# Softmax weights of both attentions turned by VectorE and moved through HBM, with the values a unit later

## The chip, the cores and the metric

One NeuronCore of a Trainium2 chip runs the kernel alone. The metric is device microseconds of one launch. The engines are named as in the profile: PE is TensorE, DVE is VectorE, ACT is ScalarE, POOL is GpSimd, SP is SyncE, whose queue issues nearly all DMAs here. Every engine, SP included, runs its own instructions strictly in the order in which the program was built: an instruction that waits holds back all that stands behind it on that engine.

## The reference

Two layers, 256 tokens, model width 1024, float32. In each layer the input is normalised, multiplied by one wide matrix, and given to three token mixers; a squared-ReLU MLP follows.

```python
for l in range(DEPTH):                                    # DEPTH = 2
    h = rms_norm(x, attn_norm[l])
    x = x + hybrid_mixer(h, ...)
    h = rms_norm(x, mlp_norm[l])
    x = x + squared_relu_mlp(h, w_mlp_up[l], w_mlp_down[l])
return rms_norm(x, final_norm)

# hybrid_mixer
p = h @ w_in
(cq, ckv, k_rope, mq, mk, mv, rq, rk, rv, rg, g_mla, g_moba, g_ret) = split(p)
o_mla  = mla_branch(cq, ckv, k_rope, ...)       # causal softmax attention, 8 heads
o_moba = moba_branch(mq, mk, mv, ...)           # with 256 tokens one block: causal softmax attention, 8 heads
o_ret  = retention_branch(rq, rk, rv, rg, ...)  # 4 heads, decay in place of softmax, group norm
merged = (sigmoid(g_mla) * (o_mla @ w_branch_mla) + sigmoid(g_moba) * (o_moba @ w_branch_moba)
          + sigmoid(g_ret) * (o_ret @ w_branch_ret))
return merged @ w_out
```

An attention head needs its softmax weights with the keys on the partitions before they can be multiplied with the values: the weights have to be turned.

## The kernel before

**Weights.** All weights stream from HBM in blocks of 512 KB (a unit): SP issues the load of `raw`, ACT rounds it to `whi` (L222), DVE subtracts to `wlo` (L224), and PE multiplies in three passes (L243 to L245), 12 matmuls of 128x512 to a unit. There are 7 buffers of `raw` and 6 each of `whi` and `wlo`. The order of the units is the plan in `weight_plan`; the names used here are those of the plan: `gmla`, `gmoba`, `gret` are the gates of the three mixers (two halves of four units each, `gmoba1.2` being the third unit of the second half), `bmla`, `bmoba`, `bret` the branch matrices (two units to a half), `rqk` (four units), `rv` and `rg` the retention's projections.

**Accumulators.** PE has four banks for `acc` and for the attention's output `po` together, taken in turn, so a unit that opens a new accumulator waits for the engine that empties the one four places earlier; and four banks for scores and the like.

**Attention.** Each attention is worked in two groups of four heads. For a group PE makes the scores `ps_s`; DVE masks and takes the maximum (L524, L527), ACT takes the exponent (L533), DVE divides (L536, L538). Then the weights `prob` are turned, by one of two ways:

- in blocks: DVE turns each head in 32x32 squares (`turned_blocks`, L543) and 16 DMAs of 48 KB, SBUF to SBUF, put the squares in place (`moved_blocks`, L594). They all stand on SP's queue, but for the second group of MoBA, where 8 stand on ACT's queue;
- on PE: `turn` (L549) makes three transposes to a head against the identity into `ps_pt`, and ACT copies the result (L550).

The first group of the MLA attention and both groups of MoBA take the first way, the second group of MLA the second. PE then multiplies with the values (`po`, L609 and L611), and ACT and DVE split the result into `omlah`, `omlal` or `omobah`, `omobal` (L264).

**Where things stand.** A list of slots says after which unit each such job is written: `first`, `gap` and `turn` of `attention` count units from the attention's first slot. The engine order within that is made when the program is built. In layer 0 of the kernel before, PE runs gmoba0.2, the 12 transposes, gmoba0.3, gmoba1.0, gmoba1.1, the MLA values together with the first MoBA scores, gmoba1.2, gmoba1.3, bmla (four units), rqk.0, rqk.1, the second MoBA scores, rqk.2, rqk.3, rv, rg.0 to rg.3, the MoBA values with the retention's scores `ps_r`, then gret. The last matmul of rg.3 stands behind `ps_r`. Layer 1 is the same some 402 us later. `retA` (L1034) is the retention's scores times their decay table `dec`, `por` its output, `gn` its norm's weights, loaded by SP (L1101), `qkoth` a moved copy of queries or keys for the rotation (L464, DMAs, and POOL or DVE at L476 and L479).

Of the kernel before, what the change touches and what calls it, by code (L numbers as in the profile page):

```python
# [7 lines left out]
F32 = mybir.dt.float32  # L8
# [6 lines left out]
P = 128  # L15
D = 1024
S = 256
# [45 lines left out]
def weight_plan():  # L63

    plan = []

    def block(key, name, kt, cols, per):
        for j in range(0, kt, per):
            plan.append(((*key, j // per), name, (j, per), cols))

    def turned(key, cols):
        for n in range(4):
            block((*key, n), "w_in", KD, cols[P * n : P * n + P], KD)

    def span(c, n):
        return range(c, c + n)

    for l in range(L):
        if l == 0:

            for i in range(2):
                plan.append(((l, "mq", i), "w_in", (0, 1), C_MQ[256 * i : 256 * i + 256]))
            plan.append(((l, "b0", 0), "w_in", (0, 1), C_MLA))
            for k in range(1, KD):
                plan.append(((l, "b0mq", k), "w_in", (k, 1), [*C_MLA, *C_MQ]))
        else:
            block((l, "b0"), "w_in", KD, C_MLA, 2)
            turned((l, "mq"), C_MQ)
        turned((l, "mk"), C_MK)
        block((l, "mv"), "w_in", KD, C_MV, 2)  # L90
        mv, plan = plan[-4:], plan[:-4]
        for i, (key, name, kt, cols) in enumerate(
            (("qrope", "mla_w_q_up", 2, C_QROPE), ("qnope", "mla_w_q_up", 2, C_QNOPE), ("kvup", "mla_w_kv_up", 1, C_KV))
        ):
            block((l, key), name, kt, cols, kt)
            plan.append(mv[i])
        plan.append(mv[3])
        for i in range(2):
            block((l, "gmla%d" % i), "w_in", KD, span(C_GMLA + 512 * i, 512), 2)
        for i in range(2):  # L100
            block((l, "gmoba%d" % i), "w_in", KD, span(C_GMOBA + 512 * i, 512), 2)
        def branch_block(name, i):
            block((l, "b%s%d" % (name, i)), "w_branch_" + name, 4, span(512 * i, 512), 2)

        for i in range(2):
            branch_block("mla", i)
        turned((l, "rqk"), C_RQK)
        block((l, "rv"), "w_in", KD, C_RV, 2)
        block((l, "rg"), "w_in", KD, span(C_RG, 512), 2)
        for i in range(2):  # L110
            block((l, "gret%d" % i), "w_in", KD, span(C_GRET + 512 * i, 512), 2)
        for name, i in LATE:
            branch_block(name, i)
        for n in range(KD):
            block((l, "wout", n), "w_out", KD, span(P * n, P), KD)
        for kind, i in mlp_order():
            if kind == "up":
                g, j = divmod(i, 4)
                plan.append(((l, "up", g, j), "w_mlp_up", (2 * j, 2), span(512 * g, 512)))
            else:  # L120
                plan.append(((l, "down", i, 0), "w_mlp_down", (i, 1), range(D)))
    at, offset = {}, 0
# [26 lines left out]
def trunk(ctx: ExitStack, tc: tile.TileContext, gx, wts, consts, gfin, gn, xtok, out):  # L149
# [83 lines left out]
    def misc_tile(name="misc"):  # L233
        return ps.tile([P, 512], F32, name=name, tag="misc", bufs=4)
# [281 lines left out]
    def attention_head(scale):  # L516


        got = {}

        def scores(s_ps):
            p = sb.tile([P, 3 * P], F32, name="prob", bufs=4)
            m = small("smx")
            nc.vector.tensor_tensor_reduce(  # L524
                p[:, 0:P], s_ps[:, 0:P], mask[:, P : 2 * P], 1.0, NEG_INF, ALU.add, ALU.max, m[:, 0:1]
            )
            nc.vector.tensor_tensor_reduce(  # L527
                p[:, P : 3 * P], s_ps[:, P : 3 * P], mask, 1.0, NEG_INF, ALU.add, ALU.max, m[:, 1:2]
            )
            nc.vector.tensor_scalar(m[:, 2:4], m[:, 0:2], -scale, None, op0=ALU.mult)  # L530
            spans = ((0, P), (P, 3 * P))
            for i, (a, b) in enumerate(spans):
                nc.scalar.activation(  # L533
                    p[:, a:b], p[:, a:b], AF.Exp, bias=m[:, 2 + i : 3 + i], scale=scale, accum_out=m[:, 4 + i : 5 + i]
                )
            nc.vector.reciprocal(m[:, 6:8], m[:, 4:6])  # L536
            for i, (a, b) in enumerate(spans):
                nc.vector.tensor_scalar(p[:, a:b], p[:, a:b], m[:, 6 + i : 7 + i], None, op0=ALU.mult)  # L538
            got["p"] = p

        def turn_blocks(dst):

            return nc.vector.transpose(dst, got["p"])  # L543

        def turn(dst):

            pt = misc_tile("ps_pt")
            for i, src in enumerate((0, P, 2 * P)):
                nc.tensor.transpose(pt[:, P * i : P * i + P], got["p"][:, src : src + P], ident)  # L549
            return lambda: nc.scalar.activation(dst, pt[:, : 3 * P], AF.Copy)  # L550

        return scores, turn_blocks, turn

    def attention(oT, vs, scale, first, group, former, gap, turn, homes):

# [5 lines left out]
        def four_tile(h):  # L561
            if h // 4 not in tiles:
                tiles[h // 4] = sb.tile([P, 4 * 3 * P], F32, name="probT", bufs=2)
            return tiles[h // 4]
# [12 lines left out]
                tc.keep_in_program_order(turning)  # L577
            pT[h] = o[:, 0:2], o[:, 2]

        def turned(h):  # L580

            o = four_tile(h)[:, 3 * P * (h % 4) : 3 * P * (h % 4) + 3 * P]
            pT[h] = o[:, 0:S], o[:, S : 3 * P]
            return heads[h][2](o)

        def moved_blocks(h0):


            e = 3 * P
            for a in range(4):  # L590
                for b in range(4):
                    src = pT["blocks"][32 * a : 32 * a + 32, e * b : e * b + e]
                    queue = nc.scalar if h0 and b % 2 else nc.sync
                    dma = queue.dma_start(four_tile(h0)[32 * b : 32 * b + 32, e * a : e * a + e], src)  # L594
                    if former:
                        tc.keep_in_program_order(dma)

        def values(h0):

# [27 lines left out]
        at(first, lambda: in_a_row(*former, lambda: four(0)))  # L627
        at(first + gap, lambda: in_a_row(lambda: four(4)))
        for i in range(2):
            if homes[i] is None:  # L630
                at(first + turn[i], lambda i=i: in_a_row(*(lambda h=h: turned(h) for h in range(4 * i, 4 * i + 4))))
                continue
            for h in range(4):
                at(first + turn[i] + h // 2, lambda h=4 * i + h: turned_blocks(h, heads[h][1]))
            at(first + turn[i] + 1, lambda i=i: moved_blocks(4 * i))
# [91 lines left out]
    def at(slot, step):  # L727
        steps.setdefault(slot, []).append(step)
# [12 lines left out]
    def layer(l, xn, before):  # L741
# [222 lines left out]
        def mla_scores(h0):  # L964
# [3 lines left out]
                    nc.tensor.matmul(bank[:, o], mla["Q"][:, h, qs], mla["K"][:, h, ks], start=True, stop=True)  # L968
            return banks

        mla_last = attention(
            omlaT, lambda: mla["v"], QKD**-0.5, first, mla_scores, (), MLA_GAP, MLA_TURN, ("probT", None)
        )


# [3 lines left out]
        def load_dec():  # L979

            rqkv["dec"] = sb.tile([P, K_TURNED_MB - K_DEC], F32, name="dec", tag="Q", bufs=1)
            tc.keep_in_program_order(nc.sync.dma_start(rqkv["dec"], consts[:, K_DEC:K_TURNED_MB]))

        at(slot("gmoba1", 3), load_dec)
        merged, mT = {}, []
        branch(l, "bmla", range(2), omlaT, th_mla, merged)
        if l == 0:

            for i, (key, j) in enumerate((("gmoba0", 0), ("gmoba0", 1), ("gmoba1", 0), ("gmoba1", 1))):
                at(slot(key, j), lambda i=i: moba_rope(("mk", "mq")[i % 2], i // 2))  # L990
        first = slot("gmoba1", 1)
        at(first, lambda: omobaT.extend((t4("omobah"), t4("omobal"))))

        def moba_scores(h0):
# [6 lines left out]
            return banks  # L1001

        moba_last = attention(
            omobaT, lambda: mqkv["mv"], MB_D**-0.5, first, moba_scores, mla_last, GAP, TURN, ("KK", "KK")
        )


# [74 lines left out]
                split_turned(oret_T[0], oretT)  # L1082

        project_turned(l, "rqk", xn, ret_pair)
        project(l, "rv", xn, 512, ret_done("rv"))


# [38 lines left out]
        branches = {"moba": (omobaT, th_moba), "ret": (oretT, th_ret)}  # L1126
        for name, half in LATE:
            branch(l, "b" + name, [half], *branches[name], merged, between if name == "ret" else None)
        at(slot("rg", 1), lambda: in_a_row(*moba_last, ret_scores))
        for h in range(RT_H):  # L1130
            at(slot("rg", 3), lambda h=h: ret_values(h))
        at(slot("rg", 3), group_norm)
        at(slot("rg", 3), oret_blocks)
        at(slot("bmoba1", 1), oret_split)


# [235 lines left out]
GAP = 8  # L1372
# [87 lines left out]
```

## Time and profile before

| what | value |
|---|---|
| median of 3 runs | 815.7 us (815.59 to 816.0) |
| profiled execution | 816.03 us |
| its span | 814.1 us |
| granted TensorE clock | 0.999 |
| PE busy | 807.1 us, 99% of the span |
| DVE, ACT, POOL busy | 577.3 us (71%), 459.9 us (56%), 98.2 us (12%) |

The span is the profiled execution without 1.9 us that lie around it. An engine's busy share is a mean over the whole span; what holds the end is read from the chain that ended last, which follows the last instruction back through what released it.

### The profile page before, as it was taken

What the parts mean: (1) busy time and instruction counts of PE and PEld (TensorE: products, weight loads), DVE (VectorE), ACT (ScalarE), POOL (GpSimd) and SP (SyncE); (2) the same over time, 40 slices, a digit from 0 to 9 for tenths busy, and PEclk for the clock granted to TensorE, in tenths of its full rate; (3) what the DMA queues carried; (4) which work ended last, traced back from release to release, by engine and by line L of the source; (5) the groups of instructions that cost most, each with busy time, mean ns of one, the idle gap of its engine ahead of it and who ended that gap; (6) DMA issues with size and microseconds to landing.
All of it is one profiled execution on the core that took longest, in us unless ns stands there. A gap on an engine that the chain in (4) does not pass through costs nothing.

```text
span 814.1 us, 11424 instructions
## 1 busy us (share of the span) xinstructions
PE 807.1 (99%) x3991; PEld 677.1 (83%) x3991; DVE 577.3 (71%) x950; ACT 459.9 (56%) x722; POOL 98.2 (12%) x75
## 2 busy tenths in 40 slices
PE   9999999999999999999999999999999999999996
PEld 7888888888888888888899888888888888888885
DVE  6879599798786455555598985886898754665554
ACT  7676655445555455555586565645546645555551
POOL 0100440330030000000035221012201200000000
PEclk9999999999999999999999999999999999999999
DMA  9964665767476777776657539448674676898731
GB/s 334 350 232 133 223 219 190 254 217 271 143 224 214 236 256 259 260 256 236 212 176 218 180 107 367 143 130 282 219 239 162 219 242 227 294 301 282 255 133 52
DMA packets 65528, 182.14 MB, mean 224 GB/s; under 512 B 9024, under 2 KB 23744, under 8 KB 65216
## 3 DMA queue, kind: packets, MB, share of 16 engines
q1 hardware_dynamic: 64128, 179.97, 65.8%
q10 hardware_dynamic: 1344, 1.46, 0.6%
q8 instruction: 31, 0.51, 0.3%
q14 instruction: 25, 0.20, 0.1%
HBM read 161.47 MB, written 11.53 MB: 213 GB/s over the span
## 4 chain that ended last, share of the span: by engine, by line
PE 99%; DVE 0%; ACT 0%; issue 0%; DVEq 0%
PE acc L245 18%; PE acc L243 18%; PE acc L244 18%; PE pup L244 7%; PE pup L243 7%; PE pup L245 7%; PE acc L1150 6%; PE acc L442 5%; PE acc L444 2%; PE ps_s L968 1%; PE acc L810 1%; PE po L609 1%; PE ps_s L511 1%; PE warm L721 0%; PE acc L812 0%; PE po L611 0%
## 5 line engine op out<-in xcount | busy, mean ns | idle before, releaser
L224 DVE TENSOR_TENSOR wlo<-raw,whi 128x1024 fp32r<-128x1024 f32 (+4 forms) x287 | 340.6, 1206 | 107.1 <-ACT whi L222 104.7
L222 ACT ACTIVATE whi<-raw 128x1024 fp32r<-128x1024 f32 (+4 forms) x287 | 287.7, 1022 | 167.7 <-PE acc L245 89.6
L243 PE MATMUL acc<-whi,xs 128*128 128x512 f32 (+1 forms) x304 | 118.5, 391 | 0.0
L245 PE MATMUL acc<-whi,xs 128*128 128x512 f32 (+1 forms) x304 | 118.4, 389 | 0.0
L244 PE MATMUL acc<-wlo,xs 128*128 128x512 f32 (+1 forms) x304 | 117.8, 387 | 0.0
L244 PE MATMUL pup<-wlo,xs 128*128 128x512 f32 x256 | 99.8, 390 | 0.0
L243 PE MATMUL acc<-whi,sq 128*128 128x512 f32 x256 | 99.8, 390 | 0.0
L245 PE MATMUL pup<-whi,xs 128*128 128x512 f32 x256 | 99.6, 389 | 0.0
L245 PE MATMUL acc<-whi,sq 128*128 128x512 f32 x256 | 99.6, 389 | 0.0
L244 PE MATMUL acc<-wlo,sq 128*128 128x512 f32 x256 | 99.6, 389 | 0.0
L243 PE MATMUL pup<-whi,xs 128*128 128x512 f32 x256 | 99.3, 389 | 0.0
L264 DVE TENSOR_TENSOR sq<-hturned,sq 128x1024 fp32r<-128x1024 f32 x16 | 19.6, 1225 | 75.5 <-ACT sq L264 75.5
L243 PEld LDWEIGHTS acc<-whi,xs 128*128 128x128 f32 x304 | 57.0, 188 | 11.5 <-issue 0.7
L245 PEld LDWEIGHTS acc<-whi,xs 128*128 128x128 f32 x304 | 57.1, 188 | 11.4
L244 PEld LDWEIGHTS acc<-wlo,xs 128*128 128x128 f32 x304 | 57.1, 188 | 11.0
L264 ACT ACTIVATE sq<-hturned 128x1024 fp32r<-128x1024 f32 x16 | 17.0, 1060 | 79.6 <-DMA hturned<-bounce 79.6
L243 PEld LDWEIGHTS acc<-whi,sq 128*128 128x128 f32 x256 | 48.1, 188 | 10.0
L245 PEld LDWEIGHTS acc<-whi,sq 128*128 128x128 f32 x256 | 48.1, 188 | 10.0
L244 PEld LDWEIGHTS acc<-wlo,sq 128*128 128x128 f32 x256 | 48.0, 188 | 9.9
L245 PEld LDWEIGHTS pup<-whi,xs 128*128 128x128 f32 x256 | 48.1, 188 | 9.8
L244 PEld LDWEIGHTS pup<-wlo,xs 128*128 128x128 f32 x256 | 48.1, 188 | 9.7
L243 PEld LDWEIGHTS pup<-whi,xs 128*128 128x128 f32 x256 | 47.9, 188 | 9.8
(216 smaller groups left out, 1137.5 us busy)
## 6 DMA issues: line engine op xcount, KB each, us to landing
raw<-wts SPq DMA_DIRECT2D x264, 512.0 KB, 4.6
bounce<-hblocks SPq DMA_DIRECT2D x16, 512.0 KB, 4.7
hturned<-bounce SPq DMA_DIRECT2D x64, 128.0 KB, 2.9
probT<-blocks SPq DMA_DIRECT2D x80, 48.0 KB, 2.0
qkoth<-qkraw SPq DMA_DIRECT2D x48, 64.0 KB, 2.4
raw<-wts SPq DMA_DIRECT2D x5, 464.0 KB, 6.0
dec<-consts SPq DMA_DIRECT2D x2, 1024.0 KB, 6.6
raw<-wts SPq DMA_DIRECT2D x4, 416.0 KB, 4.1
```

What stands on the lines that cost most here:

```text
L222: fetched.append(nc.scalar.activation(hi[:, cs], raw[:, cs], AF.Copy))
L224: nc.vector.tensor_sub(lo[:, cs], raw[:, cs], hi[:, cs].bitcast(F32))
L243: nc.tensor.matmul(o, ah, bh, start=start, stop=False, **more)
L244: nc.tensor.matmul(o, ah, bl, start=False, stop=False, **more)
L245: nc.tensor.matmul(o, al, bh, start=False, stop=stop, **more)
L264: return nc.scalar.activation(hi, src, AF.Copy), nc.vector.tensor_sub(lo, src, hi.bitcast(F32))
L442: nc.tensor.matmul(acc, wh[:, k, :], xn.both(k), start=k == 0, stop=False)
L444: nc.tensor.matmul(acc[:, 0:S], wl[:, k, :], xn.k(k)[0], start=False, stop=k == KD - 1)
L511: mm = nc.tensor.matmul(bank[:, o], a[rows, sa], b[rows, sb_], start=True, stop=True)
L609: nc.tensor.matmul(dst, vh, pT[h + j][0], start=True, stop=False)
L810: nc.tensor.matmul(mq[n], wq[n][0], xn.both(k), start=k == 0, stop=False)
L1150: nc.tensor.matmul(o, a, b, start=half == 0 and i == 0, stop=4 * half + n == KD and i == len(jobs) - 1)
```

## The change

Five things are changed.

1. The second group of MLA is turned as the others are, by DVE in blocks; the transposes on PE and their copies on ACT are gone, in both layers.
2. All four groups of a layer are put in place through HBM: one write of the turned squares (768 KB) to `pbounce` and four reads of 192 KB back. All five stand on SP's queue, ACT's queue issues none.
3. The plan puts the four units of rqk ahead of bmla, and the program likewise. The last read of each attention's second group is put ahead of the load of a named unit (`behind[last]`): rqk.3 in layer 0, bmla0.1 in layer 1 for MLA, gret0.2 for MoBA. The load of `dec` goes behind the last MLA read.
4. The MLA values with the first MoBA scores move from after gmoba1.1 to after gmoba1.2 (`first`).
5. The MoBA values with `ps_r` are written at the slot of rg.2 where rg.1 was, and `por`, the norm and its turning at gret0.0 where rg.3 was.

```diff
@@ weight_plan
+        turned((l, "rqk"), C_RQK)
         for i in range(2):
             branch_block("mla", i)
-        turned((l, "rqk"), C_RQK)
@@ attention_head
-        def turn(dst):
-            pt = misc_tile("ps_pt")
-            for i, src in enumerate((0, P, 2 * P)):
-                nc.tensor.transpose(pt[:, P * i : P * i + P], got["p"][:, src : src + P], ident)
-            return lambda: nc.scalar.activation(dst, pt[:, : 3 * P], AF.Copy)
@@ attention
-            for a in range(4):
-                for b in range(4):
-                    src = pT["blocks"][32 * a : 32 * a + 32, e * b : e * b + e]
-                    queue = nc.scalar if h0 and b % 2 else nc.sync
-                    dma = queue.dma_start(four_tile(h0)[32 * b : 32 * b + 32, e * a : e * a + e], src)
+            tile_ = four_tile(h0)
+            bounce = dr.tile([P, 4 * e], F32, name="pbounce", bufs=2)
+            dmas = [nc.sync.dma_start(bounce, pT["blocks"])]
+            for b in range(4):
+                src = bounce.rearrange("(a p) (b r) -> b p a r", a=4, b=4)[b]
+                dst = tile_[32 * b : 32 * b + 32].rearrange("p (a r) -> p a r", a=4)
+                dmas.append(nc.sync.dma_start(dst, src))
+            if h0:
+                behind[last] = dmas[-1:]
@@ mla_last
-            omlaT, ..., MLA_GAP, MLA_TURN, ("probT", None)
+            omlaT, ..., MLA_GAP, MLA_TURN, ("probT", "KK"), mla_next    # (l,"bmla0",1) if l else (l,"rqk",3,0)
@@ load_dec
-        at(slot("gmoba1", 3), load_dec)
+            with tc.issue_after(behind[mla_next][0].ins): ...
-        branch(l, "bmla", range(2), omlaT, th_mla, merged)
-        first = slot("gmoba1", 1)
+        first = slot("gmoba1", 2)
@@ after project_turned(l, "rqk", xn, ret_pair)
+        branch(l, "bmla", range(2), omlaT, th_mla, merged)
+        at(slot("rqk", 0), load_dec)
@@
-        at(slot("rg", 1), lambda: in_a_row(*moba_last, ret_scores))
+        at(slot("rg", 2), lambda: in_a_row(*moba_last, ret_scores))
-            at(slot("rg", 3), lambda h=h: ret_values(h))
+            at(slot("gret0", 0), lambda h=h: ret_values(h))
```

`group_norm` and `oret_blocks` move from the slot of rg.3 to that of gret0.0 in the same way.

What the engines run at one place of layer 0, from the second MoBA group to the start of gret, on three engines. First SP before: the second group's 8 moves on this queue stand behind 11 weight loads, 16 moves and 8 of `qkoth`, and two weight loads (gret0.2, gret0.3) stand ahead of `gn`.

```order
33 L207 DMA raw<-wts 128x1024 x11
34 L594 DMA probT<-blocks 32x384 x16
35 L464 DMA qkoth<-qkraw 32x512 x8
36 L594 DMA probT<-blocks 32x384 x8
37 L207 DMA raw<-wts 128x1024 x2
38 L1101 DMA gn<-gn 128x1024
39 L207 DMA raw<-wts 128x1024 x13
```

And SP after, the same place:

```order
39 L464 DMA qkoth<-qkraw 32x512 x4
40 L207 DMA raw<-wts 128x1024
41 L579 DMA pbounce<-blocks 128x1536
42 L583 DMA probT<-pbounce 32x4x384 x4
43 L579 DMA pbounce<-blocks 128x1536
44 L583 DMA probT<-pbounce 32x4x384 x4
45 L1089 DMA gn<-gn 128x1024
46 L207 DMA raw<-wts 128x1024 x15
```

The raw load ahead of the first write is gret0.1; gret0.2, gret0.3 and gret1.0 are the first three of the 15 behind `gn`, and all of them stand behind the second group's write and reads.

ACT before, from the retention's values `rv` on; the units rounded ahead of the first `omobah` are gret0.0, gret0.1 and gret0.2, and gret0.3 and gret1.0 follow.

```order
118 L1013 ACTIVATE rv<-acc,ms 128x512 x2
119 L222 ACTIVATE whi<-raw 128x1024 x2
120 L1092 ACTIVATE rg<-acc,half 128x512
121 L222 ACTIVATE whi<-raw 128x1024
122 L264 ACTIVATE omobah<-po 128x512
123 L222 ACTIVATE whi<-raw 128x1024
124 L264 ACTIVATE omobah<-po 128x512
125 L222 ACTIVATE whi<-raw 128x1024
126 L1092 ACTIVATE rg<-acc,half 128x512
```

And ACT after, first of layer 0 and then of layer 1:

```order
120 L999 ACTIVATE rv<-acc,ms 128x512 x2
121 L222 ACTIVATE whi<-raw 128x1024 x3
122 L264 ACTIVATE omobah<-po 128x512
123 L222 ACTIVATE whi<-raw 128x1024
124 L264 ACTIVATE omobah<-po 128x512
125 L1080 ACTIVATE rg<-acc,half 128x512
```

```order
316 L222 ACTIVATE whi<-raw 128x1024 x3
317 L999 ACTIVATE rv<-acc,ms 128x512 x2
318 L222 ACTIVATE whi<-raw 128x1024 x4
319 L264 ACTIVATE omobah<-po 128x512 x2
320 L1080 ACTIVATE rg<-acc,half 128x512
```

In layer 0 the three units ahead of the first `omobah` are now gret0.1, gret0.2 and gret0.3, in layer 1 the four are gret0.1 to gret1.0.

DVE at the same place before, the second group's weights having been turned already:

```order
229 L479 TENSOR_TENSOR qkT<-qkT,qkoth 128x512 x2
230 L224 TENSOR_TENSOR wlo<-raw,whi 128x1024 x2
231 L1093 SCALAR_TENSOR_TENSOR rg<-rg,acc 128x512
232 L224 TENSOR_TENSOR wlo<-raw,whi 128x1024
233 L264 TENSOR_TENSOR omobal<-po,omobah 128x512
234 L224 TENSOR_TENSOR wlo<-raw,whi 128x1024
235 L264 TENSOR_TENSOR omobal<-po,omobah 128x512
```

And DVE after, layer 0:

```order
245 L543 STREAM_TRANSPOSE blocks<-prob 128x3x4x32
246 L224 TENSOR_TENSOR wlo<-raw,whi 128x1024
247 L543 STREAM_TRANSPOSE blocks<-prob 128x3x4x32
248 L224 TENSOR_TENSOR wlo<-raw,whi 128x1024 x4
249 L264 TENSOR_TENSOR omobal<-po,omobah 128x512
250 L224 TENSOR_TENSOR wlo<-raw,whi 128x1024
251 L264 TENSOR_TENSOR omobal<-po,omobah 128x512
```

The unit between the last two turns is rg.3, the four behind them are gret0.0 to gret0.3; in layer 1 both turns stand ahead of rg.3, and gret1.0 too stands ahead of `omobal`.

## Rows read from the trace of the kernel before

**Rows 1.** The page, chain that ended last: share of the span by engine.

```profile
PE 99%; DVE 0%; ACT 0%; issue 0%; DVEq 0%
```

**Rows 2.** Chain in order of time: start us, us, what; both layers' transposes.

```profile
91.38 1.31 PE ps_pt L549 x12
...
493.60 1.31 PE ps_pt L549 x12
```

**Rows 3.** Timeline, PE (start us, us, instruction): MLA values, rv.0, MoBA values, gret0.0; last, layer 1's gret0.0.

```profile
100.81 0.65 PE L609 MATMUL po<-probT,vml 128*64 128x256 f32 x4
...
134.40 0.40 PE L243 MATMUL acc<-whi,xs 128*128 128x512 f32 x1
...
156.05 0.65 PE L609 MATMUL po<-probT,mv 128*64 128x256 f32 x4
...
160.64 0.39 PE L243 MATMUL acc<-whi,xs 128*128 128x512 f32 x1
...
562.88 0.39 PE L243 MATMUL acc<-whi,xs 128*128 128x512 f32 x1
```

**Rows 4.** Timeline, DVE, layer 0: kinds of instruction that stand in its queue there.

```profile
85.16 0.55 DVE L538 TENSOR_SCALAR prob<-prob,smx 128x128 f32<-128x128 f32 x2
...
117.07 3.49 DVE L224 TENSOR_TENSOR wlo<-raw,whi 128x1024 fp32r<-128x1024 f32 x3
120.48 1.28 DVE L675 SCALAR_TENSOR_TENSOR th<-th,acc 128x512 f32<-128x512 f32 x2
...
131.06 0.27 DVE L524 CUSTOM_DVE_ANT_0 prob<-ps_s,K 128x128 f32<-128x128 f32 x1
...
131.61 0.28 DVE L524 CUSTOM_DVE_ANT_0 prob<-ps_s,K 128x128 f32<-128x128 f32 x1
...
132.16 0.69 DVE L476 TENSOR_TENSOR qkT<-qkraw,tab 128x512 f32<-128x512 f32 x1
...
136.63 0.16 DVE L536 RECIPROCAL smx<-smx 128x2 f32<-128x2 f32 x1
136.82 0.55 DVE L538 TENSOR_SCALAR prob<-prob,smx 128x128 f32<-128x128 f32 x2
...
141.59 1.96 DVE L543 STREAM_TRANSPOSE blocks<-prob 128x384 f32<-128x384 f32 x4 [0.35 <-issue]
```

**Rows 5.** Timeline, DVE and POOL, layer 0: a DVE instruction beside a POOL one.

```profile
144.57 1.77 DVE L476 TENSOR_TENSOR qkT<-qkraw,tab 128x512 f32<-128x512 f32 x1
...
144.19 1.61 POOL L476 TENSOR_TENSOR qkoth<-qkoth,tab 128x512 f32<-128x512 f32 x1 [28.05 <-DMA qkoth<-qkraw]
```

**Rows 6.** DMA issues at 382.6, 298.6, 652.5, 151.0, 151.7 and 152.1: KB each, us to landing.

```profile
bounce<-hblocks SPq DMA_DIRECT2D x1, 512.0 KB, 3.3
...
bounce<-hblocks SPq DMA_DIRECT2D x1, 512.0 KB, 5.8
...
hturned<-bounce SPq DMA_DIRECT2D x4, 128.0 KB, 2.8
...
raw<-wts SPq DMA_DIRECT2D x1, 512.0 KB, 4.2
...
gn<-gn SPq DMA_DIRECT2D x1, 512.0 KB, 6.6
...
raw<-wts SPq DMA_DIRECT2D x1, 512.0 KB, 7.6
```

**Rows 7.** Timeline, SP's queue: the first MLA group's moves; the four reads of a bounce.

```profile
74.72 10.04 SPq L594 DMA_DIRECT2D probT<-blocks  x16
...
652.55 1.75 SPq L279 DMA_DIRECT2D hturned<-bounce  x4
```

**Rows 8.** Timeline, ACT and DVE, layer 0: the MoBA output taken from PE.

```profile
157.62 0.60 ACT L264 ACTIVATE omobah<-po 128x512 fp32r<-128x512 f32 x1 [0.22 <-PE po L611]
158.11 1.05 ACT L222 ACTIVATE whi<-raw 128x1024 fp32r<-128x1024 f32 x1
...
158.57 0.68 DVE L264 TENSOR_TENSOR omobal<-po,omobah 128x512 fp32r<-128x512 f32 x1
```

More of the change, by code (lines that the diff above doesn't have):

```diff
@@ L543, in turn_blocks, with attention @@
             return nc.vector.transpose(dst, got["p"])
-        def turn(dst):
-            pt = misc_tile("ps_pt")
-            for i, src in enumerate((0, P, 2 * P)):
-                nc.tensor.transpose(pt[:, P * i : P * i + P], got["p"][:, src : src + P], ident)
-            return lambda: nc.scalar.activation(dst, pt[:, : 3 * P], AF.Copy)
-        return scores, turn_blocks, turn
-    def attention(oT, vs, scale, first, group, former, gap, turn, homes):
+        return scores, turn_blocks
+    def attention(oT, vs, scale, first, group, former, gap, turn, homes, last):
         tiles, pT = {}, {}
@@ L578, in turned_blocks @@
             pT[h] = o[:, 0:2], o[:, 2]
[L580 to L584, printed above, removed]
         def moved_blocks(h0):
             e = 3 * P
-            for a in range(4):
-                for b in range(4):
-                    src = pT["blocks"][32 * a : 32 * a + 32, e * b : e * b + e]
-                    queue = nc.scalar if h0 and b % 2 else nc.sync
-                    dma = queue.dma_start(four_tile(h0)[32 * b : 32 * b + 32, e * a : e * a + e], src)
-                    if former:
-                        tc.keep_in_program_order(dma)
+            tile_ = four_tile(h0)
[7 more added lines that the diff above has]
+                behind[last] = dmas[-1:]
         def values(h0):
@@ L629, in attention @@
         for i in range(2):
-            if homes[i] is None:
-                at(first + turn[i], lambda i=i: in_a_row(*(lambda h=h: turned(h) for h in range(4 * i, 4 * i + 4))))
-                continue
             for h in range(4):
@@ L969, in mla_scores @@
             return banks
+        mla_next = (l, "bmla0", 1) if l else (l, "rqk", 3, 0)
         mla_last = attention(
-            omlaT, lambda: mla["v"], QKD**-0.5, first, mla_scores, (), MLA_GAP, MLA_TURN, ("probT", None)
+            omlaT, lambda: mla["v"], QKD**-0.5, first, mla_scores, (), MLA_GAP, MLA_TURN, ("probT", "KK"), mla_next
         )
@@ L981, in load_dec @@
             rqkv["dec"] = sb.tile([P, K_TURNED_MB - K_DEC], F32, name="dec", tag="Q", bufs=1)
-            tc.keep_in_program_order(nc.sync.dma_start(rqkv["dec"], consts[:, K_DEC:K_TURNED_MB]))
-        at(slot("gmoba1", 3), load_dec)
+            with tc.issue_after(behind[mla_next][0].ins):
+                tc.keep_in_program_order(nc.sync.dma_start(rqkv["dec"], consts[:, K_DEC:K_TURNED_MB]))
         merged, mT = {}, []
-        branch(l, "bmla", range(2), omlaT, th_mla, merged)
         if l == 0:
@@ L1003, in layer @@
         moba_last = attention(
-            omobaT, lambda: mqkv["mv"], MB_D**-0.5, first, moba_scores, mla_last, GAP, TURN, ("KK", "KK")
+            omobaT, lambda: mqkv["mv"], MB_D**-0.5, first, moba_scores, mla_last, GAP, TURN, ("KK", "KK"), (l, "gret0", 2)
         )
@@ L1128, in layer @@
             branch(l, "b" + name, [half], *branches[name], merged, between if name == "ret" else None)
-        at(slot("rg", 1), lambda: in_a_row(*moba_last, ret_scores))
+        at(slot("rg", 2), lambda: in_a_row(*moba_last, ret_scores))
         for h in range(RT_H):
-            at(slot("rg", 3), lambda h=h: ret_values(h))
-        at(slot("rg", 3), group_norm)
-        at(slot("rg", 3), oret_blocks)
+            at(slot("gret0", 0), lambda h=h: ret_values(h))
+        at(slot("gret0", 0), group_norm)
+        at(slot("gret0", 0), oret_blocks)
         at(slot("bmoba1", 1), oret_split)
```

## The prediction

> **What bounds the kernel now.** I read the chain that ended last first: 99% of it is PE [rows 1], and its list in order of time holds nothing but matmuls back to back. So a microsecond taken from PE's own work is gained, and a microsecond taken from DVE, ACT or a queue is worth nothing until PE has to wait for it. Second, the same chain around the second MLA group: the block of 12 transposes is a piece of 1.31 us in each layer [rows 2]. That is what can be won. Third, where PE meets the attention's results: the timelines of PE, DVE, ACT and SP from the second MoBA group to gret0.0 [rows 3, 4, 8], since there the change moves most.
>
> **Removed from PE.** The 24 transposes: 2 x 1.31 = 2.62 us [rows 2]. No matmul is added. Their copies on ACT lay off the chain, as ACT has no share in it [rows 1], and give nothing.
>
> **Added to DVE.** Four turns to a layer, 1.96 us for four [rows 4]. For MLA they lie under PE's gates of MoBA: the last division of the second group ends at 85.7, the turns at 87.7, a write of 4.1 and reads of 4.5 (worked out below) make 96.3, and PE wants these weights at 100.81 + 2.73 - 1.31 + 1.4 = 103.6: one unit later than before (2.73, below), less the transposes, and half of `po` further on. Cover 7 us, so nothing. If that cover were gone, each microsecond late would be one of PE's.
>
> **Moved: weights.** rqk.3 and `dec` wait on SP for those reads. Eight `qkoth` issues at about 0.6 (the 16 moves of the same kind of queue took 10.04, [rows 7]) put rqk.3 at about 101.5; with the 1 MB of `dec` ahead (two blocks of 1.4) and a load of 4.2 [rows 6] it lands by 108.5, `whi` and `wlo` are done by 111, and PE comes to it at about 118. Covered.
>
> **Moved: the accumulators at bmla0.** bmla0.0 now opens the bank of rqk.0, which DVE empties behind the first MoBA softmax. DVE has, from about 105 on, two outputs of MLA (1.3), four heads (2.2), four `wlo` (4.6), four divisions (2.8), two turns (1.0) and the emptying (0.4), priced by [rows 4]: 12.3, so 117.3, against PE's 120.7. Cover 3.4 us; a rival below eats it.
>
> **Moved: the MoBA values, and what stands ahead of taking them.** Here I expect the loss, so it is worked step by step; times are on the clock of the trace, without any new wait.
>
> PE: from rv.0 at 134.40 to `po` at 156.05 are 95 matmuls [rows 3], 0.228 us each, 2.73 a unit. gret0.0 follows the same work as before but for the transposes: 160.64 - 1.31 = 159.33 in layer 0, 562.88 - 2.62 = 560.26 in layer 1. Back from it: rg.3 now stands between (2.73), `po` and `ps_r` take 4.59 less one matmul, 4.36, so `po` starts at 152.2; nine units and the second scores (1.5) earlier, at 126.2, bmla0 ends.
>
> DVE, from there to the last turn of the second MoBA group, has no gap in its order: six `wlo` at 1.16, four gate products at 0.64, one sum at 0.69, six turns at 0.49, four heads at 0.55, four reciprocals with divisions at 0.71 [rows 4]. Together 18.2, so 144.5. In layer 1 rg.3's `wlo` stands behind the turns: 17.0, from 527.1, so 544.2. One POOL instruction falls into that stretch, and beside one a DVE instruction of 0.69 took 1.77 [rows 4, 5]: between 0 and 1.08; I take 0.5, since DVE waits for the POOL result soon after anyway. So 145.0 and 544.7.
>
> Write: 768 KB to HBM were never made here. The write of 512 KB took 3.3 with little beside it and 5.8 among loads [rows 6]. SP's queue is empty of loads at that point, so I take the quiet row; the 256 KB more cost 0.7, half of the 1.4 by which a load of 512 KB landed behind `gn` (152.10 + 7.6 against 151.73 + 6.6). With 0.1 to issue, 4.1: 149.1 and 548.8. Bounds 3.7 and 6.5.
>
> Reads: the four issue over 1.75, the last some 1.3 after the first [rows 7], and take 2.8 [rows 6]; 0.3 for the larger size and 0.1 for the wait give 4.5: 153.6 and 553.3. PE wants the second group's weights at 152.2 + 1.4 = 153.6. A tie, and a wait there only uses up part of the next one.
>
> Behind the reads SP has `gn`, gret0.2, gret0.3, gret1.0. `gn` landed 3.1 behind the load ahead of it (151.02 + 4.2); a plain load of its size needs 1.4. I take 2.3. The loads behind it 1.4 each. Layer 0: `gn` 155.9, gret0.3 158.7. Layer 1: 555.6, gret1.0 559.8.
>
> ACT and DVE: before, one `whi` and one `wlo` stood between PE's `po` and its taking over, all of weights landed long ago, and the take-over followed `po` at once [rows 8]. After, the `whi` of gret0.3 (layer 1: of gret1.0) stands ahead of `omobah`, and its `wlo` ahead of `omobal`. From landing: 0.1 + 1.05 [rows 8], 1.16, 0.64 and 0.1 to PE make 3.05. So the first `po` bank is free at 161.75 in layer 0 and 562.85 in layer 1. gret0.0 opens just that bank and stands ready at 159.33 and 560.26: PE waits 2.4 and 2.6 us. The second bank (behind gret1.0's `wlo` in layer 0) comes free by 163.4, wanted at 163.8: no more is lost.
>
> Sum: 2.4 + 2.6 - 2.62 = +2.4 us. Against the profiled execution's 816.03 that is 818.4; the median stands 0.3 below it, so **818.1 us**. Bounds of the two waits: with no POOL collision, a write of 3.7, and `gn` at 1.4 each shrinks by 1.8, to 0.6 and 0.8 (814.5); with 1.08, a write of 5.0 and 3.1 each grows by 2.4 (822.9).
>
> A rule of the Trainium skill speaks against this loss: "DMA: Bandwidth & Descriptors", section "Rules for kernel authors", asks to coalesce many small transfers, as those under 64 KB are mostly overhead. The 16 moves are 48 KB each. On the issue time the trace agrees (10.04 us for 16 [rows 7]); on the whole way to the values no row here shows it. What it would give is the first rival.
>
> **The rivals.**
>
> *Faster: the weights behind are early enough.* SP spent 10.04 us on 16 moves [rows 7] and spends about 2.2 on five issues now. If the write and the reads return sooner than I add up, gret0.3 lands before PE has finished rg.3, ACT and DVE keep pace with `po`, and only the transposes count: 815.7 - 2.6 = 813.1. It needs the landings 2.4 and 2.6 us earlier than in the sum. For it: the saving in issues is real. Against it: before, the last moves needed no round trip through HBM and the two loads were issued right after them; now they wait for the write to land first, 4 us in which SP does nothing else. The order decides at the landing of gret0.3: before about 156.2 nothing is lost.
>
> *Same: half the wait.* Each wait is half as long (DVE a microsecond earlier, `gn` like a plain load): 2.5 - 2.6, so 815.6.
>
> *Slower still: POOL on the first MoBA softmax.* POOL turns MoBA's queries and keys in layer 0 with six instructions; if they fall on DVE's softmax as the one in [rows 5] fell on a product, 6 x 1.08 = 6.5 eat the cover of 3.4 at bmla0: 3.1 more, 821.2. Against it: their data come earlier than before, as the reads cost fewer issues than the moves.
>
> *That the change does not do what it says* is small: the order lists show no transposes, and the units stand as written.
>
> **How the numbers follow.** A measurement of this kernel can tell about 0.2%, 1.6 us, from no change: faster is below 814.1, slower above 817.3. The forecast, a wait of 4.3 to 7.5 us in all, gets 0.41; half the wait (1.0 to 4.3) 0.33; no wait 0.19; POOL on top 0.07. Slower is then 0.48, same 0.33, faster 0.19. The likeliest case's own range is 817.3 to 820.5. The range for 8 in 10 has to take in half the wait and nearly all of no wait: 813.2 to 820.8.
>
> **What would show it.** Right: PE busy a little under the old 99% share; two waits of PE, at gret0.0 of each layer, released by DVE's `omobal`; ahead of them on ACT a `whi` released by the landing of `raw`, while `po` has long ended; gret0.3 landing near 158.7 in layer 0. The weights of gret0.2 issued not before 151. Wrong: no wait of PE there (then the landings are earlier, and the step that failed is the write, the reads or `gn`), or waits at bmla0 or at `po` instead (then DVE's or the reads' sum failed). The transposes' 2.62 us should be missing from PE's work in any case.

## The result: slower by 8.6 us

The changed kernel takes 824.25 us (median of 4 runs, 823.52 to 825.5) against 815.64 for the kernel before, a ratio of 1.0107, 95% interval 1.0089 to 1.0124. The forecast was 818.1 with a range up to 820.8: the side was right, the size was not.

**Profile after.** The page of the changed kernel, its busy times and its chain; PE's share of the chain was 99% [rows 1].

```profile
PE 807.0 (98%) x3967; PEld 675.1 (82%) x3967; DVE 570.7 (69%) x958; ACT 454.5 (55%) x714; POOL 95.3 (12%) x75
...
PE 91%; DMA 4%; DVE 2%; SPq 1%; issue 1%; ACT 0%; DVEq 0%; ACTq 0%
```

The list of waits, changed kernel, PE (us in total, times, longest). Before, PE waited for nothing after its start.

```profile
PE po L598 <- DMA probT<-pbounce: 5.2, 2, 3.4
PE acc L243 <- DVE omobal L264: 2.8, 2, 2.5
```

So the loss sits at two places of each layer: the second heads of the MoBA values, which wait for the reads, and gret0.0, which waits for the bank that these values leave (in layer 0 nearly all the waiting is at the first, in layer 1 at both). Timeline of the changed kernel: PE at both places in layer 0, then ACT and DVE ahead of gret0.0 in layer 1.

```profile
157.10 1.12 PE L598 MATMUL po<-probT,mv 128*64 128x256 f32 x4 [3.37 <-DMA probT<-pbounce]
...
164.71 0.50 PE L243 MATMUL acc<-whi,xs 128*128 128x512 f32 x1 [0.25 <-DVE omobal L264]
...
567.60 1.06 ACT L222 ACTIVATE whi<-raw 128x1024 fp32r<-128x1024 f32 x1 [0.17 <-DMA raw<-wts]
568.57 1.07 ACT L264 ACTIVATE omobah<-po 128x512 fp32r<-128x512 f32 x2
...
569.84 1.28 DVE L264 TENSOR_TENSOR omobal<-po,omobah 128x512 fp32r<-128x512 f32 x2
```

The first line also shows the clock: four matmuls took 1.12 us where they took 0.65 in [rows 3]. The stretches of the changed kernel (length; PE, PEld, DVE, ACT, POOL busy; then granted clock, DMA share, GB/s) show at which clock PE went on:

```profile
153.40:157.10 3.70, 0.33 (x7) 0.12 (x3) 0.00 (x0) 0.00 (x0) 0.00 (x0) 0.93 1.02 243
157.10:160.00 2.90, 2.90 (x18) 1.94 (x18) 0.00 (x0) 0.00 (x0) 0.00 (x0) 0.50 1.00 364
...
560.00:562.10 2.10, 0.31 (x8) 0.10 (x5) 0.00 (x0) 0.00 (x0) 0.00 (x0) 1.00 0.99 298
562.10:565.00 2.90, 2.90 (x32) 2.37 (x32) 0.00 (x0) 0.00 (x0) 0.00 (x0) 1.00 1.01 403
```

After the pause of layer 0 the clock was granted at 0.50, the 1.2 GHz level, for 2.9 us; after the shorter one of layer 1 it stayed at 1.00. The sum over both layers, by the starts of PE's matmuls (3.65 us between where the second heads would have started and where they did; the profile counts 3.37 of them as idle): in layer 0 the values wait 3.65 us and their second half takes 2.75 instead of 1.4, rg.3 with the wait behind it 3.3 instead of 2.9; in layer 1 the values take 4.76 instead of 2.75, and rg.3 with its wait 5.56 instead of 2.9. That is 10.1 us; less 2.6 for the transposes, 7.5, and the span grew by 7.6 (821.7 against 814.1).

**Where it begins.** Timeline of the changed kernel, DVE in layer 0, the POOL instruction it waits for, DVE in layer 1; L476 and L479 are the products and the addition of retention's rotation.

```profile
124.83 0.69 DVE L476 TENSOR_TENSOR qkT<-qkraw,tab 128x512 f32<-128x512 f32 x1
129.20 0.69 DVE L479 TENSOR_TENSOR qkT<-qkT,qkoth 128x512 f32<-128x512 f32 x1 [3.68 <-POOL qkoth L476]
...
127.89 1.28 POOL L476 TENSOR_TENSOR qkoth<-qkoth,tab 128x512 f32<-128x512 f32 x1 [16.73 <-DMA qkoth<-qkraw]
...
534.63 0.69 DVE L479 TENSOR_TENSOR qkT<-qkT,qkoth 128x512 f32<-128x512 f32 x1 [4.97 <-DMA qkoth<-qkraw]
```

DVE stands 3.7 and 5.0 us, in order, ahead of the first of a layer's two additions, for the exchange of halves of retention's turned q and k (the `qkoth` moves, 4 of 64 KB). Behind it stand the rest of the first MoBA group, the whole second softmax and its turns. The DMA issues of the changed kernel at 121.3, 148.0 and 151.2 (KB each, us to landing): the exchange, the write and the four reads of the second group.

```profile
qkoth<-qkraw SPq DMA_DIRECT2D x4, 64.0 KB, 5.2
...
pbounce<-blocks SPq DMA_DIRECT2D x1, 768.0 KB, 3.2
...
probT<-pbounce SPq DMA_DIRECT2D x4, 192.0 KB, 3.5
```

DVE's last turn in layer 0 (timeline), and the chain that ended last, in order of time, from there to gret0.0 (start us, us, what):

```profile
147.43 0.56 DVE L543 STREAM_TRANSPOSE blocks<-prob 128x384 f32<-128x384 f32 x1
```

```profile
148.02 3.18 DMA pbounce<-blocks
...
154.02 7.61 DMA raw<-wts
161.73 1.07 ACT whi L222
162.82 0.52 DVE wlo L224
...
163.97 0.69 DVE omobal L264
164.71 0.50 PE acc L243
```

The last turn ends at 147.99 (551.41 in layer 1), the write has landed at 151.19, the last read at 156.96. The chain runs over the load of gret0.3 (154.02) and not over `po`: when gret0.0 starts is set by the landing of that load, so what PE loses at the values, the clock included, in layer 0 only uses up the wait at gret0.0. In the kernel before, the order of DVE has both additions of the rotation behind the four turns at 141.59 [rows 4]; the change put rqk, and with it the rotation, ahead of bmla and so ahead of them.

### The profile page after: what moved, and what is told of

Same layout as the page of the kernel before. It is cut to its first block, busy times and chain, and to the rows that moved or that the text cites. A ratio compares the mean times of both kernels' runs of the same rounds, so it can differ in the third digit from the quotient of the medians.

```text
span 821.7 us, 11301 instructions
## 1 busy us (share of the span) xinstructions
PE 807.0 (98%) x3967; PEld 675.1 (82%) x3967; DVE 570.7 (69%) x958; ACT 454.5 (55%) x714; POOL 95.3 (12%) x75
## 4 chain that ended last, share of the span: by engine, by line
PE 91%; DMA 4%; DVE 2%; SPq 1%; issue 1%; ACT 0%; DVEq 0%; ACTq 0%
PE acc L243 16%; PE acc L245 16%; PE acc L244 16%; PE pup L245 7%; PE pup L243 7%; PE pup L244 7%; PE acc L1138 5%; PE acc L442 4%; DMA raw<-wts 3%; PE acc L444 2%; PE ps_s L954 1%; PE acc L796 1%; DVE wlo L224 1%; DMA pbounce<-blocks 1%; DMA qkoth<-qkraw 1%
```

## The experiments

Theory A: DVE's wait for retention's exchange, which the new order puts ahead of the second softmax, makes everything behind it late. Rivals: B, the trip through HBM is too long whenever it starts; C and E, the order of rqk and bmla, or the unit by which the scores came later, as such; P, the place of the values; D, the first attention's own trip. All edits are to the changed kernel.

**1. The exchange issued by ACT.**

```diff
-            dma = nc.sync.dma_start(other[a : a + 32, :], raw[b : b + 32, :])
+            dma = queue.dma_start(other[a : a + 32, :], raw[b : b + 32, :])
```

(`queue` is ACT's for retention, SP's elsewhere.)

> The exchanges of halves (qkoth) of retention's turned q and k are issued by ACT instead of SP, so they no longer stand on SP's queue behind the loads of rg; all else is as in the changed kernel. Theory A (the late start of VectorE: it stood 3.7 us in the first layer and 5.0 us in the second for these exchanges, and everything behind it came so much later): the last turn ends about 144.5 and 546.7, the write and the reads keep their 3.2 to 3.9 and 5.7 to 6.5 us, the second heads wait under 0.5 us and gret0.0 under 0.7 us: of the 10.4 us lost at these four places about 9 come back, time 814 to 817. Rival B (the round trip through HBM is too long whenever it starts): reads and the weights behind them stay late, time over 820. Rival C (VectorE's order after the swap of rqk and bmla): no change, about 824.

823.5 us, ratio 1.0103 [1.0081, 1.0126]: nothing gained. The exchange's DMA issues and DVE's wait in this kernel:

```profile
qkoth<-qkraw ACTq DMA_DIRECT2D x4, 64.0 KB, 5.9
```

```profile
130.26 0.69 DVE L480 TENSOR_TENSOR qkT<-qkT,qkoth 128x512 f32<-128x512 f32 x1 [4.14 <-DMA raw<-wts]
```

The edit did not take the wait away, so it decides nothing between A and B; it shows that SP's queue alone is not what holds the exchange. SP's loads were still in flight beside it.

**2. Moves for MoBA, and 3. loads free to go ahead of the reads.** In 2, `moved_blocks` issues the 16 moves of before when it serves MoBA. In 3:

```diff
-            if h0:
+            if h0 and last[1] != "gret0":
                 behind[last] = dmas[-1:]
```

> The second attention's two groups are put in place by the 16 moves of 48 KB of the kernel before (8 of the second group's on ACT) and not through HBM; the first attention still goes through HBM, places in the program as in the changed kernel. Theory A (late start of VectorE): the last turn stays at 148.0, eight moves a queue at 0.64 us and 2 us to land end at about 155.2, so the second heads still wait about 1.7 us in the first layer; the weights of gret0 are no longer behind reads, so the waits at gret0.0 go: time 815.5 to 818.5. Rival B (the round trip is the cause): all 10.4 us come back, 812.5 to 814. Rival C (order of VectorE): 822 to 825.

> Only one rule is taken out: the load of gret0.2 may now be issued ahead of the second attention's four reads. Theory A: the wait at gret0.0 in the second layer (2.8 us, for the weights of gret1.0 that landed at 567.50, ACT's whi of them and the omobah behind it) goes, and the 0.6 us in the first layer; the 3.6 and 2.0 us at the second heads stay or grow by up to 1.2 us a layer, one load ahead of the reads: time 820 to 823. Rival B (the trip alone): the wait at the second heads grows and takes back all, 824 to 826.

825.6 us, 1.0104 [1.0071, 1.0137], and 827.4 us, 1.0146 [1.0131, 1.0161]. Both came out above every expectation; for run 2 the order of DVE (C) was nearest. PE's waits in run 3, and the write of the second group there:

```profile
PE po L598 <- DMA probT<-pbounce: 11.1, 2, 7.6
```

```profile
pbounce<-blocks SPq DMA_DIRECT2D x1, 768.0 KB, 6.8
```

Loads ahead of the write and the reads made them 6.8 and 6.3 us long instead of 3.2 and 5.7: putting the reads ahead of later weights pays here. In run 2 the idle time of DVE at the exchange was 4.1 us and the last move landed 10.6 us after the last turn, behind the loads of gret0.2 to gret1.1. Its edit passes over the rule of run 3 as well, and so lets these loads go ahead of the moves: run 2 alone does not refute B.

**4. Only the first attention's part.** Moves for MoBA, its values and retention's steps in their old places, bmla ahead of rqk again:

```diff
-        at(slot("rg", 2), lambda: in_a_row(*moba_last, ret_scores))
+        at(slot("rg", 1), lambda: in_a_row(*moba_last, ret_scores))
```

> Only the first attention's part of the change: its second group is turned by VectorE and goes through HBM, its values a unit later; the second attention's moves, places and the order of loads are those of the kernel before. Theory A and rival B both: only the 12 transposes a layer go, the cover of the first attention holds, time 812.5 to 814.5. Rival D (the first attention's own trip costs too, hidden so far under the second's loss): 815 to 817.

829.4 us, 1.0175 [1.0158, 1.0193], 15 us beyond A and B and 12 beyond D. PE's waits, one in each layer; the last move lands just ahead of the end of each:

```profile
PE po L605 <- ACT whi L222: 6.7, 1, 6.7
PE po L605 <- DMA probT<-blocks: 5.7, 1, 5.7
```

Here, too, the second group is late: MoBA's scores are still a unit later, retention's addition is ahead of the second pair of turns in DVE's order (idle 2.6 us there), the first group's moves end at 148.2 and the last turn at 150.3 (before: 143.5). So the transposes' gain can't be had by undoing the rest alone.

**5. No exchange at all.** Retention is turned without its exchange of halves, which leaves that part of the computation out.

```diff
-        other = swapped(raw, late)
+        other = w2k("qkoth") if plain else swapped(raw, late)
```

> Leaves part of the computation out: retention's q and k are turned without the exchange of their halves, so the 8 exchange DMAs (qkoth) of each layer and VectorE's wait for them are gone; all else as in the changed kernel. Theory A (VectorE stands 3.7 and 5.0 us for these exchanges because retention's rotation now lies ahead of the second softmax in its order): last turn about 144.3 and 546.5, reads in by 153.5 and 557, waits at the second heads under 0.5 us, at gret0.0 under 1 us: 814 to 817. Rival B (the round trip through HBM is too long whatever the start): over 820.

817.4 us, 1.0022 [1.0011, 1.0034]: 6.8 of the 8.6 us come back. Last turns at 144.4 and 546.0. PE's waits:

```profile
PE acc L243 <- DVE omobal L264: 2.1, 2, 1.4
PE po L598 <- DMA probT<-pbounce: 1.0, 1, 1.0
```

A holds, 0.4 us over its span; B falls: the trip is the same.

**6 to 8. MoBA's scores a unit earlier, alone; with bmla ahead of rqk; and with MoBA's moves and old places as well.**

```diff
-        first = slot("gmoba1", 2)
+        first = slot("gmoba1", 1)
...
-        at(first, lambda: in_a_row(*former, lambda: four(0)))
+        at(first, lambda: in_a_row(lambda: four(0)))
+        at(first + 1, lambda: in_a_row(*former))
```

> The second attention's scores and turns stand one unit earlier, where the kernel before had them; the first attention's values stay a unit later; all else as in the changed kernel, rqk still ahead of bmla, so retention's rotation is still ahead of the second pair of turns in VectorE's order. Theory A (the rotation's wait): the wait stays, last turn still after 147, time 821 to 825. Rival E (it is the unit by which the scores came later): last turn near 144, 815 to 818.

> As the last one, and bmla again ahead of rqk in the list of weights and in the program: every softmax still goes through HBM, the first attention's values still come a unit later, but retention's rotation falls behind the second group's last turn in VectorE's order, as in the kernel before. Theory A: last turn about 143, write 3.5 and reads 6 land at 152.5 to 153, no wait at the second heads (wanted at 153.5), gret0.0 waits 0 to 1 us for the weights behind the reads: 813 to 816.5. Rival B (the round trip): over 819.

> The first attention's part of the change alone: its second group turned by VectorE and taken through HBM, its values a unit later; the second attention keeps its moves, its scores' place, its values' place; bmla ahead of rqk. Theory A: only the 24 transposes go, 812.5 to 814.5. Rival D (the first attention's trip or its outputs, now behind the second softmax on VectorE, hold up bmla0): 815.5 to 819.

821.3 us, 1.0067 [1.0052, 1.0082]; 822.4, 1.0077 [1.0059, 1.0095]; 824.3, 1.0103 [1.0088, 1.0118]. The first is in A's range (last turn 146.9, just under the 147 of A; DVE idle 1.9 at the exchange). But PE's waits there are not all of A's kind: 2.6 us at gret0.0, and

```profile
PE ps_s L511 <- POOL qkT L479: 1.9, 1, 1.9
PE acc L442 <- DVE omlal L264: 1.0, 2, 0.5
```

The 1.9 us and half of the 1.0 lie in layer 0 ahead of the last turn and may have made it later, so run 6 does not rule out E; run 9 does. The other two missed A's range, and not at the place in question: in 7 the time lies where B put it, but the last turn ends at 144.9 and the values do not wait. PE's waits in 7, then in 8:

```profile
PE acc L243 <- DVE omlal L264: 3.8, 2, 2.0
PE ps_s L511 <- POOL qkT L479: 3.4, 1, 3.4
```

```profile
PE acc L243 <- DVE omlal L264: 5.9, 2, 3.4
PE ps_s L511 <- POOL qkT L479: 2.5, 1, 2.5
```

The earlier scores wait for POOL's rotation of MoBA's q and k in layer 0, and bmla0, next behind the later MLA values, for the output of these values, which DVE takes behind the softmax: in 8 the place that D named, at 5 us over D's range. In the changed kernel the later scores and rqk ahead of bmla cover these two places; their price is the halt at the exchange.

**9. The additions of the rotation held behind the last turn.** The cause alone, with the whole computation; `behind["turn"]` is the last turn of the group.

```diff
-            rT.append(rope_turned(raw, rqkv["tab"], nc.vector))
+            other = swapped(raw)
+            at(
+                slot("rv", 3),
+                lambda: rT.append(rope_turned(raw, rqkv["tab"], nc.vector, other=other, after=behind["turn"])),
+            )
...
-        engine.tensor_add(o, o, other)
+        with tc.issue_after(after.ins) if after else ExitStack():
+            engine.tensor_add(o, o, other)
```

> The whole computation, with one change to the changed kernel: the two additions that end retention's rotation, which wait for the exchanged halves, are held behind the last turn of the second group on VectorE. Theory A (their wait is what delays the second group): the idle time of 3.7 and 5.0 us is gone, last turn 143.5 to 144.5 and 545 to 546, waits of PE 1.5 to 3.1 us in all instead of 8.0, time 814.5 to 817.5, as in the run without exchanges. Rival B (the gain there came from fewer DMAs, not from the wait): the wait goes and the time stays over 819.

815.1 us, 0.9994 [0.9986, 1.0003]: the 8.6 us are back. Last turns at 143.1 and 544.6. DVE's last turn in layer 0 and, behind it, both additions without a wait (timeline):

```profile
142.51 0.57 DVE L544 STREAM_TRANSPOSE blocks<-prob 128x384 f32<-128x384 f32 x1
143.00 1.25 DVE L480 TENSOR_TENSOR qkT<-qkT,qkoth 128x512 f32<-128x512 f32 x2
```

All that PE waits for is

```profile
PE acc L243 <- DVE omobal L264: 2.4, 2, 1.4
```

The edit holds nothing but two additions a layer; a few neighbours shifted by some places with them (two exponents ahead of a `whi` on ACT, turns and `wlo` on DVE). The trip through HBM, rqk ahead of bmla and the later scores are all kept, so B, C and E fall as causes of their own; and run 5 took the same wait away by another edit. So A is shown. What run 9 gains over run 5, 2.3 us, was not taken apart: the additions' own 1.25 us have left the stretch too.

**10. And `gn` two units later.** Its load, its two products and the group norm:

```diff
-        at(slot("rg", 0), load_gn)
+        at(slot("gret0", 2), load_gn)
+        at(slot("gret0", 2), weighed)
-        at(slot("gret0", 0), group_norm)
-        at(slot("gret0", 0), oret_blocks)
+        at(slot("gret0", 2), group_norm)
+        at(slot("gret0", 2), oret_blocks)
```

(`weighed` holds the two products that stood in `rg_done`.)

> As the last one, and the load of gn, its two products on GpSimd and the group norm come two units later, so that gn (2.2 us of the queue) stands behind gret0.2 and gret0.3. Theory A with its second step (gret0.0 waits because the weights of gret0.3 land late behind reads and gn, ACT's whi of them and omobah): these land 2.2 us earlier, the first layer's wait at gret0.0 goes, the second layer's (on gret1.0, still behind gn) stays at 0.5 to 1 us: 813.5 to 816, about 1 us under the last one. Rival F (the group norm is on the path): slower than the last one by 1 to 4 us.

813.3 us, 0.9973 [0.9964, 0.9982]: faster than both kernels, and 0.2 under what was expected. PE's busy time on the page, and the one wait that is left, at the start:

```profile
PE 804.4 (99%) x3967; PEld 673.8 (83%) x3967; DVE 574.8 (71%) x958; ACT 455.1 (56%) x714; POOL 94.2 (12%) x75
```

```profile
PE warm L709 <- PEq L1452: 0.8, 1, 0.8
```

PE's work is 2.7 us less than before (807.1), the span 2.9: the transposes, whole. That both layers' waits went is more than was expected; the reads, with less beside them, ended at 151.8 instead of 153.2.

**11. MoBA's values behind rg.3.**

```diff
-        at(slot("rg", 2), lambda: in_a_row(*moba_last, ret_scores))
+        at(slot("rg", 3), lambda: in_a_row(*moba_last, ret_scores))
```

> Only the place of the second attention's values: one unit later than in the changed kernel, behind rg.3, where the kernel before had them. Theory A: the waits of 3.4 and 1.8 us at the second heads fall to under 1 us, but gret0.0 opens the bank that the values leave, and that comes free when it did, at about 165 to 166 and 570.5: the loss moves there, time 822 to 825. Rival P (the place of the values is the cause): 816 to 819.

825.4 us, 1.0119 [1.0105, 1.0134], 0.4 over what A said; P falls. The wait moved to gret0.0:

```profile
PE acc L243 <- DVE rg L1081: 8.5, 2, 4.8
PE po L598 <- DMA probT<-pbounce: 0.6, 1, 0.6
```

**12. Run 9 with MoBA's groups by 16 moves each.** It sets the moves beside the trip through HBM with DVE's wait out of the way; the edits are those of 9 and 2, so the rule of run 3 goes here too, and ACT issues 8 of the second group's moves.

> The additions held behind the last turn, as in the first of these runs, and the second attention's groups put in place by 16 moves each, not through HBM. It prices the round trip with VectorE's wait out of the way. Theory A: the trip itself costs little, within 2 us of the first of these runs, 813 to 817. Rival B (the trip costs its own several us): 3 us or more under the first of these runs.

818.8 us, 1.0042 [1.0027, 1.0058]: 3.7 us over run 9, on the other side from B and outside A's 2 us. SP's queue and DVE in this kernel (timeline), from the first group's moves to the second group's turns; then the first group's write in run 9:

```profile
129.48 13.08 SPq L584 DMA_DIRECT2D probT<-blocks  x16
...
144.31 1.96 DVE L544 STREAM_TRANSPOSE blocks<-prob 128x384 f32<-128x384 f32 x4 [3.04 <-DMA probT<-blocks]
```

```profile
pbounce<-blocks SPq DMA_DIRECT2D x1, 768.0 KB, 7.8
```

Both groups are turned in one buffer, `blocks`. The second group's turns wait until all 16 moves of the first have left it (143.9); one write leaves it at 136.2. What PE then waits for, and ACT's first instruction behind its moves (timeline):

```profile
PE acc L243 <- DVE rg L1094: 3.2, 1, 3.2
```

```profile
153.93 0.69 ACT L1008 ACTIVATE rv<-acc,ms 128x512 f32<-128x512 f32 x1 [12.97 <-DMA probT<-blocks]
```

The values did not wait. ACT stood 13.0 us for and among its moves, rounded five units behind them, and gret0.0 of layer 0 waited for what came after. So the trip through HBM is the faster way in this kernel; how much of the 3.7 us is the moves' own, how much ACT's queue and how much the loads that now go ahead, was not separated. The rule of the Trainium skill that the prediction weighed ("DMA: Bandwidth & Descriptors", section "Rules for kernel authors") asks to coalesce many small transfers into one large one. The trace agrees in direction: 13.08 us pass from the first to the last of the 16 issues.

**13. Loads held back from the exchange.** Why it lands so late was still open after run 1.

```diff
             rT.append(rope_turned(raw, rqkv["tab"], nc.vector))
+            behind[l, "rg", 1 + 2 * i] = list(swaps)
```

(`swaps` are the four DMAs of the exchange.)

> In the changed kernel the load of rg.1 may not be issued before retention's first exchange (4 DMAs of 64 KB), nor that of rg.3 before the second; VectorE's order stays, the additions stand where they stood. Theory G (the exchange lands 5 to 7 us after its issue because loads of 512 KB that were issued just ahead are in the way): it lands 2 to 2.5 us after its issue, VectorE's idle time falls from 3.7 and 5.0 us to under 1, time 815 to 817.5. Rival H (such an exchange takes that long at this place whatever is loaded): idle time stays over 3 us, time 821 to 825.

819.1 us, 1.0044 [1.0029, 1.0059]. The first exchange of layer 0, DVE behind it, and PE's waits:

```profile
qkoth<-qkraw SPq DMA_DIRECT2D x4, 64.0 KB, 2.0
```

```profile
127.35 0.69 DVE L483 TENSOR_TENSOR qkT<-qkT,qkoth 128x512 f32<-128x512 f32 x1 [1.19 <-POOL qkoth L480]
```

```profile
PE po L602 <- DMA probT<-pbounce: 2.4, 1, 2.4
PE acc L243 <- DVE omobal L264: 2.2, 1, 2.2
```

The landing is as G said, 2.0 us against 5.2: the loads ahead made it late. The time is not: 1.2 to 1.5 us of idle time stay, the second exchange still lands behind rg.1 and rg.2, and the last turn (146.6) gains 1.4 us, not 3.7.

## Why the prediction was right in its side and wrong in its size

- **Transposes, 2.62 us: right.** Run 10, without waits, shows 2.7 of PE's busy time and 2.9 of the span.
- **MLA's values, rqk.3, `dec`, the accumulators at bmla0: covered, as predicted.** The reads landed at 99.1 (predicted 96.3, wanted at 103.6: 2.8 us late, inside the cover), rqk.3 at 106.9 (108.5), bmla0.0 started at 120.4 without a wait. The POOL rival did not come.
- **PE's places: right.** bmla0 ended at 125.9 (126.2), `po` started at 152.20 (152.2).
- **DVE's stretch to the last turn, which "has no gap in its order": this step failed.** The 18.2 us of work were right: from the first gate product at 129.81 to the last turn at 147.99 are 18.18. Their start was not. The prediction let them begin when bmla0 ends, at 126.2; but in DVE's order the first addition of the rotation stands just ahead of them, and what that addition waits for was not asked. The exchange was taken as landed. The halt of 3.7 us in layer 0 put the last turn 3.0 late, and the one in layer 1, less 5.4 for what layer 0 had lost, 1.3. Runs 5 and 9 took the halt away and gave 817.4, which is near the forecast of 818.1, and 815.1.
- **Write: put a little too high.** 3.2 and 3.9 us (4.1, with 3.7 as the lower bound). **Reads: put too low.** 5.7 and 6.6 us from the first issue to the last landing (4.5). The row they came from was for 128 KB each [rows 6]; these are 192 KB. With the write the last read came 3.4 us late in layer 0 (halt 3.0, write -0.9, reads 1.3) and 3.3 in layer 1 (1.3, -0.2, 2.1): in layer 1 the reads, mis-sized, weigh more than the halt.
- **The tie at `po`: wrong, by the halt and the reads.** PE waited 3.65 and 2.0 us there, which the prediction gave as the sign that DVE's or the reads' sum had failed; both had. "A wait there only uses up part of the next one" held: in layer 0 the wait at gret0.0 shrank to 0.4. The clock at 0.50 behind the pause, 1.35 us, was not foreseen either, but it too came out of that wait: gret0.0 started 3.08 us behind the landing of its weights, as in layer 1, where the clock stayed at 1.00.
- **From the weights to gret0.0: right.** gret0.3 landed at 161.63 and PE went on at 164.71; gret1.0 at 567.50 and 570.58: 3.08 both times (3.05). `gn` took 2.2 and 1.8 (2.3), a load 1.25 (1.4). The waits it gives are the predicted ones, on later landings: gret0.3 came 2.9 us late, gret1.0, less the 5.4 of layer 0, 2.3.
- **The sum.** By the start of gret0.0, layer 0 lost 5.4 us instead of 2.4, layer 1 4.9 instead of 2.6: the 2.9 and 2.3 us by which the landings came late. Without the halt, run 9 leaves 2.4 us of waits at gret0.0 and lands at 815.1, where the rival "half the wait" stood.
- **The rival "faster" (813.1):** its condition was that the weights behind come early enough. The changed kernel does not meet it; run 10 does, by two more edits, and takes 813.3.

## What to carry to other kernels

When a change moves a step ahead in a list, look for what else is issued with it on in-order engines: here two additions that wait for a small transfer came ahead of a softmax, and taking their halt away gave back 6.8 and 9.1 us (runs 5 and 9), where the transposes are worth 2.6. In pricing a stretch of an engine's queue, go through it instruction by instruction and ask of each what it waits for; its duration alone is not its price. A small exchange that someone waits for belongs ahead of the large loads (run 13, 5.1 us back), or its consumer behind everything that doesn't need it (run 9, all of it).

## What the runs showed of the hardware

- An exchange of four 64-KB moves landed 2.0 us after issue with no load ahead (run 13, and 2.0 in the kernel before at 140.2), 5.2 and 6.9 behind loads of 512 KB, and 5.9 when ACT's queue issued it, beside SP's loads (run 1).
- In the changed kernel the clock was granted at 0.50 for the 2.9 us after PE had stood 3.4 us, and at 1.00 after 1.8 us. The length of the pause alone does not tell the two apart: behind one of 2.4 us in run 13 it was 0.50 from 156.7 to 160.0, behind one of 3.2 us in run 12 it was 1.00.
- Four reads of 192 KB, 768 KB in all, took 5.5 to 8.3 us from the first issue to the last landing over the eight groups of the changed kernel; one write of the same 768 KB took 3.2 to 6.0, with 3.2 and 3.9 for the second MoBA groups, where no load was in flight. In run 9 one took 7.8 behind and beside loads.
- In run 12 ACT, which issued 8 of the second group's moves, stood 13.0 us for and among them; its next instruction started at 153.93, when the last of the 8 was issued (153.88).
